# A hybrid GLA and Mamba-2 step: low parts of the weights on VectorE, the decay of the sample states on GpSimd

## The chip, the cores and the metric

The kernel runs on one core of one Trainium2 chip, as one launch. The metric is the device time of an execution in microseconds; for the kernel before it is 1887.03 us, the median of 3 runs (1886.17 to 1887.46).

## The reference

Two layers of a decoder work on 288 tokens at once: a prompt of 256 tokens, and 8 sample sequences of 4 tokens that bring their states with them. Everything is float32. In each layer:

```
x = x + 1/2 * SwiGLU_1(RMSNorm(x))
u = RMSNorm(x);  q,k,v,g,a_lr,z,xbc,dt,gate_a,gate_b = split(u @ w_in)
GLA:  S = decay * S + k_out^T v ;  o = causal(q_in k_in^T) v + q_in S       (4 heads)
SSD:  xs,B,C = silu(causal_conv(xbc)) ; h = decay * h + dS ;                (32 heads, 4 groups)
      y = (C B^T * decays) x dt + C h + d_skip * xs ; y = RMSNorm(y * silu(z))
m = sigmoid(gate_a) * (o_gla @ w_proj_gla) + sigmoid(gate_b) * (y @ w_proj_ssm);  x = x + m @ w_out
x = x + 1/2 * SwiGLU_2(RMSNorm(x))
```

The outputs are the tokens after a last RMSNorm and the new states. The state of a sample in SSD, `state_ssm`, is 64 x 128 for each of 32 heads and 8 sequences; its new value is the old one times exp(sum of dt * A over the 4 tokens), a number per head and sequence, plus a product of the new inputs with B.

## The kernel before

**Weights.** Activations are feature-major: 8 blocks of 128 features by 288 tokens. Every weight comes in pieces of up to 8 blocks of 128 x 128 (`weights`, L169): one DMA on SP's queue into `wr` (four buffers), then `split` (L157) forms a high part `wh` by a copy on ScalarE that rounds to float32r (L160) and a low part `wl` = `wr` - `wh`, a subtraction of 128 x 1024 numbers (three buffers each). The subtraction is done by VectorE (L166) or by GpSimd (L164). Which of the two is decided as the program is written out: `pool_turn` grows by `pool_share` with each piece, and when it reaches 1, one piece goes to GpSimd. `pool_share` is 1.0 in the setup (two pieces), 0.0 in the FFNs and in the projections at the end of the mixer, `SHARE_GLA` = 0.45 in the GLA stage and `SHARE_SSD` = 0.48 in the SSD stage. `mm3` (L176) multiplies a piece: for each block the products of the high part with the high and the low part of the input (L179, L180), and after all of these the low part with the high input (L182).

**Stages of a layer.** FFN, mixer, FFN. The mixer is a generator for the GLA scan and then one for the SSD scan; at each `yield` one step of a list of independent projections (`fillers`, L498: z, g, gate_a with the GLA projection, gate_b) is written between, so that TensorE has products while the chains of the scan run. The engines each run their instructions in order; a scheduler lays the order out when the program is built, so that instructions of different stages mix on an engine.

**The SSD scan** goes over 16 head pairs j (two heads each, 128 rows). The stages that matter here:

- `stage_load(j)` brings the old states of the pair, three pairs ahead: two tiles `st` of 128 x 4 x 128, for even and odd sequences.
- `stage_h` transposes these tiles on TensorE (L144), for C.h.
- `stage_x(j)` projects and convolves the input: copies into `cbuf` (L856 ScalarE, L857 and L858 VectorE), the taps on `cacc` (L861 ScalarE, three times L863 VectorE), tanh and product (L865, L867, L871); GpSimd keeps the last rows (L882, L884).
- `stage_m(j)` makes the inputs token-major, forms the decay-weighted scores `m` (L1015 to L1019 ScalarE, L1029 VectorE), `xg` (L1023 VectorE), `xd` (L1026 GpSimd), and the packed `xpk` (L1031 ScalarE, L1032 VectorE).
- `stage_y(j)` adds the samples' part to `yos` (L1042 VectorE), multiplies outputs and states on TensorE (L1047 to L1054), adds the skip (L1056 VectorE), gates with z on GpSimd (L1062), splits the result (L1064, L1066) and adds its square on GpSimd (L1069). At its end, for both tiles `st`, TensorE forms the new part of the states in a PSUM bank (L1072, from the masked B in `bm`), and VectorE updates the tile in four instructions, one a sequence: old state times its decay `decs` plus the bank (L1076). SP's queue stores it (L1078).
- `stage_group(g)` prepares B and C of four pairs (L928, L931, L936 and others).

The order in which the loop writes them is load(j+3), x(j+2), m(j+1), filler, y(j), filler. The PSUM banks of all these products come from one ring of four (`pst`).

Of the kernel before, what the change touches and what calls it, by code (L numbers as in the profile page):

```python
# [12 lines left out]
ALU = mybir.AluOpType  # L13
# [6 lines left out]
SEQ = 256  # L20
# [21 lines left out]
SHARE_GLA = 0.45  # L42
SHARE_SSD = 0.48
# [3 lines left out]
def _constants():  # L47
    p = np.arange(128)[:, None]
    f = np.arange(128)[None, :]
    ident = (p == f)  # L50
    tri = (f >= p)
    ones = np.ones((128, 128))
    suf = (p > f)
    mid = np.where(f >= 64, (p >= 64) & (p <= f), 0).astype(float) - np.where(f < 64, (p > f) & (p <= 63), 0)
    mid = np.concatenate([mid, (p <= 63), np.ones((128, 1))], 1) / 16.0
    r = p % 32
    c32 = np.arange(32)[None, :]
    ms = np.concatenate([(r // 4 == c32 // 4) & (c32 >= r), r // 4 == np.arange(8)[None, :]], 1) / 16.0
    # packed sample rows: token n in row 32 * (n // 8) + 8 * c + n % 8, for c = 0 .. 3
    tok = lambda a: 8 * (a // 32) + a % 8  # L60
    rep = lambda a: a % 32 // 8
    n, c = tok(p), rep(p)
    seq8 = (n // 4 == np.arange(8)[None, :])
    bt = (c == 0) & (n // 4 == c32 // 4) & (c32 >= n)
    btc = (c < 2) & (n // 4 == c32 // 4) & (c32 >= n)
    sel = (c == 2) & (n == c32)
    bt4 = (c == 0) & (n // 4 == tok(f) // 4) & (n <= tok(f))
    bsuf4 = (c == 0) & (n // 4 == tok(f) // 4) & (n > tok(f))
    pk = np.concatenate([c == 0, c == 1, -1.0 * (c >= 2), -1.0 * (c % 2 == 1), -1.0 * (p % 32 == 1)], 1)
    pair = (p // 2 == np.arange(16)[None, :])  # L70
    par = (p % 2 == f // 64)
    parc = (p % 2 == rep(f))
    parts = dict(ident=ident, pair=pair, tri=tri, ones=ones, seq8=seq8, btc=btc, sel=sel, pk=pk,
                 par=par, parc=parc, suf=suf, mid=mid, ms=ms, bt=bt, bt4=bt4, bsuf4=bsuf4)
    off, cols = {}, 0
    for k, v in parts.items():
        off[k] = (cols, v.shape[1])
        cols += v.shape[1]
    arr = np.concatenate([np.asarray(v, np.float32) for v in parts.values()], 1)
    return np.ascontiguousarray(arr), off  # L80
# [3 lines left out]
NKEEP = COFF["par"][0]          # the columns kept all along; the rest is for GLA and dt  # L84
# [10 lines left out]
def tile_hybrid_step(  # L95
# [21 lines left out]
    def psf():  # L117
        """any of the seven banks of products"""
        turn[0] = (turn[0] + 1) % 7
        return psg() if turn[0] % 2 else ps.tile([128, 512], F32, name="psg", tag="t", bufs=4)[:, 0:NT]  # L120
# [12 lines left out]
    def cz_put(eng, dst, src):  # L133
        """columns of the samples' tokens to the blocks of their sequences; last axes of dst: 264, of src: 32"""
        eng.tensor_copy(out=dst[:, 0:264].rearrange("p (h x) -> p h x", x=132)[:, :, 0:128].rearrange(
            "p h (r c) -> p h r c", c=32)[:, :, :, 16:20], in_=src.rearrange("p (r h t) -> p h r t", h=2, t=4))

    def pack(eng, out, src):
        """[., 32] tokens to the packed order, four times over"""
        eng.tensor_copy(out=out.rearrange("p (r c i) -> p r c i", r=4, c=4),  # L140
                        in_=bcast(src.rearrange("p (r i) -> p r i", i=8), 2, 4))
# [27 lines left out]
    def weights(src):  # L169
        """[n * 128, m <= 128] of DRAM -> the two parts, [128, n, m]"""  # L170
        n, c = src.shape[0] // 128, src.shape[1]
        raw = wpool.tile([128, n, c], F32, name="wr", tag="wr", bufs=4)
        nc.sync.dma_start(out=raw, in_=src.rearrange("(k p) c -> p k c", p=128))
        return split(raw, [128, n, c])
# [9 lines left out]
    def blocks(srcs, x, nblk, first=None, psum=psg, after=1):  # L184
        """per 128-column block: (block, psum of every source); first() follows that many products"""
        for b in range(nblk):
            out = []
            for src in srcs:
                h, lo = early.pop(0) if early else weights(src[:, b * 128:(b + 1) * 128])
                p = psum()  # L190
                mm3(p, h, lo, x[0], x[1], True, True)
                after -= 1
                if first and after == 0:
                    first()
                out.append(p)
            yield b, out

# [10 lines left out]
    def params(l, n1):  # L208
# [18 lines left out]
        # halved: conv_w, conv_b, gla_norm, ssm_norm  # L227
# [11 lines left out]
    class Norm:  # L239
        """RMSNorm of x for the coming phase, fed block by block: x * w split in two; 1 / rms is applied later"""  # L240
# [90 lines left out]
    def mixer(l, P, norm, nxt):  # L331
        W = w_in[l]
        with tc.tile_pool(name="mx", bufs=1) as mx:
# [9 lines left out]
            # the normalised input, split  # L343
# [23 lines left out]
            # conv rows: the samples' 24, the prompt's 3; of each 24 channel blocks  # L367
# [14 lines left out]
            def dt_chain():  # L382
                # dt = softplus(dt_raw + bias), dtA = -dt * exp(a_log); rows are heads
# [20 lines left out]
                # token-major dt, dtA: [tok, (dt|dtA), tile, head]  # L404
# [10 lines left out]
                # cumulative sums within 128-token tiles, suffix sums  # L415
# [9 lines left out]
                # decays to the end: [first tile, second tile, samples]  # L425
# [4 lines left out]
                # head-major cumulative sums, to DRAM for broadcasting  # L430
# [7 lines left out]
                # decay of a sample sequence, on (head, p) partitions  # L438
# [7 lines left out]
                # decays between a sample's tokens, packed rows: of even heads, of odd heads, ones  # L446
# [25 lines left out]
            def fill_g():  # L472
                # output gate of GLA (0.5 folded into gn)
# [38 lines left out]
            pool_share[0] = SHARE_GLA  # L512
            run(gla(l, P, W, norm, X, renorm, dtc, dalt, o8))
            ysq = nacc()
            pool_share[0] = SHARE_SSD
            def proj(yh, conv_store):
                for _ in F:
                    pass
                pool_share[0] = 0.0
# [28 lines left out]
    def gated(wg, X, wp, phs, pls, done):  # L548
        """per output block: done(block, tanh of half the gate, psum of the projection)"""
# [14 lines left out]
    def gla(l, P, W, norm, X, renorm, dtc, dalt, o8):  # L564
        with tc.tile_pool(name="gla", bufs=1) as gp:
# [4 lines left out]
            # both operands of the low-rank product in parts: rows of (x_h, w_l), (x_h, w_h), (x_l, w_h)  # L570
# [8 lines left out]
            # dt and the low-rank decay input  # L579
# [12 lines left out]
            # log_a * 16, token-major  # L592
# [55 lines left out]
            # decays  # L648
# [40 lines left out]
            # sample  # L689
# [19 lines left out]
            # the samples' scores, and the sum of the rows of q.S  # L709
# [4 lines left out]
            # k_out, packed  # L714
# [13 lines left out]
            # prompt states  # L728
# [19 lines left out]
            # outputs, prompt  # L748
# [10 lines left out]
            # sample: outputs and states, two heads at a time  # L759
# [14 lines left out]
            def reads(i):  # L774
                """q.S of four sequences, on a quarter of the columns each"""
# [51 lines left out]
            # per-head RMS: 32 rows of sums per head, broadcast again after 1 / sqrt  # L827
# [19 lines left out]
    def ssd(l, P, W, X, yf, dtt, ac, dec3, eAs, decs, mse, acd, ysq, scf, cbufs, yr, yblk, proj):  # L847
# [3 lines left out]
        with tc.tile_pool(name="ssd", bufs=1) as sp_:  # L851
            def conv(pg, cb, tag, bufs):
                """conv + silu of channel block cb -> compact [128, NT] tile (times 1, weights were halved)"""
# [21 lines left out]
            def bass_sample(a):  # L875
                # the last sequence's group has 4 of 7 columns only
                v = a[:, SEQ + 3 - 3:NCV]          # 56 columns: 3 before, then 8 x (4 + 3)
                return v.rearrange("p (s t) -> p s t", t=7)[:, :, 3:7]

            def conv_last(cb, buf):  # L880
                """last three rows of every sequence, in the old state's place"""
# [12 lines left out]
            R = {}                      # what the stages hand on  # L894
# [3 lines left out]
            def stage_bc(g):  # L898
                """B and C of a group: projection and convolution"""
# [8 lines left out]
            def stage_pack(g):  # L908
                Bf, Cf = R.pop(("bc", g))
                # C of the samples, sequence by sequence  # L910
# [6 lines left out]
            def stage_group(g):  # L917
                """B token-major, C.B, the samples' packed operands"""
# [10 lines left out]
                # C.B  # L929
# [8 lines left out]
                # the samples' score matrices of 4 head pairs, and the sum of the rows of C.h  # L938
# [17 lines left out]
            def stage_load(j):  # L956
                """states of a head pair: even sequences, odd sequences"""
# [4 lines left out]
            def stage_h(hg, i):  # L962
                """C.h of the samples' states"""
# [11 lines left out]
            def stage_h2(hg, i):  # L975
                """C.h, four sequences at a time on a quarter of the columns each"""
# [15 lines left out]
            def stage_x(j):  # L992
                """projection and convolution of a head pair"""
# [9 lines left out]
            def stage_m(j):  # L1003
                """token-major inputs and the decay-weighted scores"""
# [30 lines left out]
            def stage_y(j):  # L1035
                """outputs and new states of a head pair"""
# [3 lines left out]
                y = pst()  # L1040
                for hh in range(2):
# [28 lines left out]
                for hf in range(2):  # L1070
# [3 lines left out]
                    for r in range(4):  # L1074
                        n = 8 * j + 2 * r + hf
                        V.scalar_tensor_tensor(out=sts[hf][:, r], in0=sts[hf][:, r], scalar=decs[:, n:n + 1],  # L1076
                                               in1=p[:, r * 128:r * 128 + 128], op0=ALU.mult, op1=ALU.add)
# [180 lines left out]
```

## Time and profile before

| what | value |
|---|---|
| time, median of 3 runs | 1887.03 us |
| span of the profiled execution | 1883.5 us |
| TensorE busy | 1828.2 us (97%) |
| VectorE busy | 1306.7 us (69%) |
| ScalarE busy | 1032.3 us (55%) |
| GpSimd busy | 347.8 us (18%) |
| DMA | 325.42 MB, mean 173 GB/s |

The profile is of one execution; its page gives the span, from the first to the last instruction, and no other time of that execution. The difference between the span and the median of the timed runs, 3.5 us, lies around the instructions. TensorE's busy time is modelled at the ends of its matmuls, so its gaps say more than its share. GpSimd's work lies in the scan stages (about 222 to 662 us and 1150 to 1590 us) but for the setup.

### The profile page before, as it was taken

How to read it: one execution, taken by the hardware profiler on the slowest of the kernel's cores; microseconds unless marked ns; L12 is line 12 of the kernel's file. 1: busy time of each engine (PE TensorE's matmuls, PEld its weight loads, DVE VectorE, ACT ScalarE, POOL GpSimd, SP SyncE). 2: the span in 40 equal slices, each digit the busy share in tenths (PEclk: the TensorE clock that was granted, in tenths of full speed). 3: DMA queues.
4: the chain of work that ended last, by engine and by line, in shares of the span. 5: the costliest groups of instructions: out<-in, count | busy, mean ns of one | idle time of the engine just before them, and what ended most of it. 6: DMA issues, size and time to landing. Idle time of an engine off the chain costs nothing.

```text
span 1883.5 us, 34917 instructions
## 1 busy us (share of the span) xinstructions
PE 1828.2 (97%) x13712; PEld 1757.0 (93%) x13712; DVE 1306.7 (69%) x2311; ACT 1032.3 (55%) x1818; POOL 347.8 (18%) x324
## 2 busy tenths in 40 slices
PE   8999999998999999999999999999999999999998
PEld 8999998898888899999999999998889898999997
DVE  6555587689888867555565556777988888665554
ACT  6444466565666646444454446565666665454443
POOL 1000032245455300000000001213444452000000
PEclk9999999998999999999999999999989999999999
DMA  7555554866676665555555555569567685555553
GB/s 212 166 164 158 158 154 137 251 184 180 182 202 187 170 179 174 164 169 163 169 167 161 164 164 148 141 193 254 145 168 201 182 220 165 171 159 167 166 157 95
DMA packets 613112, 325.42 MB, mean 173 GB/s; under 512 B 17090, under 2 KB 607986, under 8 KB 612948
## 3 DMA queue, kind: packets, MB, share of 16 engines
q1 hardware_dynamic: 612900, 323.07, 60.1%
q8 instruction: 107, 1.75, 0.4%
q14 instruction: 57, 0.47, 0.1%
q10 hardware_dynamic: 48, 0.13, 0.0%
HBM read 292.93 MB, written 30.22 MB: 172 GB/s over the span
## 4 chain that ended last, share of the span: by engine, by line
PE 49%; DVE 7%; ACT 3%; issue 1%; DMA 1%; POOL 0%; SPq 0%; DVEq 0%; ACTq 0%; POOLq 0%
PE psg L179 15%; PE psg L180 15%; PE psg L182 15%; DVE cacc L863 2%; DVE wl L166 1%; PE pst L144 1%; ACT wh L160 1%; DVE yos L1042 1%; ACT cacc L861 0%; DVE cbuf L858 0%; DMA acb<-acd 0%; DVE st L1076 0%; DVE o L478 0%; PE pst L792 0%; DVE m L1029 0%
## 5 line engine op out<-in xcount | busy, mean ns | idle before, releaser
L160 ACT ACTIVATE wh<-wr 128x1024 fp32r<-128x1024 f32 (+1 forms) x498 | 517.3, 1040 | 449.9 <-PE psg L180 365.6
L179 PE MATMUL psg<-xh,wh 128*128 128x288 f32 x2704 | 748.9, 303 | 9.3 <-DVE cbuf L857 2.7
L180 PE MATMUL psg<-xl,wh 128*128 128x288 f32 x2704 | 742.4, 300 | 0.1
L166 DVE TENSOR_TENSOR wl<-wr,wh 128x1024 fp32r<-128x1024 f32 (+1 forms) x413 | 502.1, 1216 | 126.5 <-ACT wh L160 126.0
L179 PEld LDWEIGHTS psg<-xh,wh 128*128 128x128 f32 x2704 | 514.2, 191 | 16.7 <-issue 6.8
L180 PEld LDWEIGHTS psg<-xl,wh 128*128 128x128 f32 x2704 | 514.9, 191 | 4.4 <-issue 1.9
L182 PE MATMUL psg<-xh,wl 128*128 128x288 f32 x2704 | 415.6, 296 | 0.0
L164 POOL TENSOR_TENSOR wl<-wr,wh 128x1024 fp32r<-128x1024 f32 x85 | 208.3, 2452 | 962.1 <-ACT wh L160 482.1
L182 PEld LDWEIGHTS psg<-xh,wl 128*128 128x128 f32 x2704 | 379.1, 189 | 0.2
L179 PE MATMUL psg<-hh,wh 128*128 128x288 f32 x704 | 189.8, 296 | 0.0
L180 PE MATMUL psg<-hl,wh 128*128 128x288 f32 x704 | 189.5, 295 | 0.0
L306 DVE TENSOR_TENSOR t<-t,psg 128x288 f32<-128x288 f32 x88 | 40.0, 454 | 135.1 <-ACT wh L160 122.9
L180 PEld LDWEIGHTS psg<-hl,wh 128*128 128x128 f32 x704 | 132.6, 188 | 0.0
L179 PEld LDWEIGHTS psg<-hh,wh 128*128 128x128 f32 x704 | 132.2, 188 | 0.1
L863 DVE SCALAR_TENSOR_TENSOR cacc<-cbuf,cw,cacc 128x312 f32<-128x312 f32 x144 | 112.6, 782 | 12.1 <-ACT cacc L861 10.5
L182 PE MATMUL psg<-hh,wl 128*128 128x288 f32 x704 | 109.2, 295 | 0.0
L303 DVE TENSOR_TENSOR t<-psg,rr 128x288 f32<-128x288 f32 x88 | 40.2, 457 | 90.5 <-PE psg L182 90.5
L182 PEld LDWEIGHTS psg<-hh,wl 128*128 128x128 f32 x704 | 99.0, 188 | 0.0
L1076 DVE SCALAR_TENSOR_TENSOR st<-st,decs,pst 128x128 f32<-128x128 f32 x256 | 72.3, 340 | 0.0
L179 PE MATMUL psg<-yh,wh 128*128 128x288 f32 x256 | 69.9, 299 | 0.2
L179 PE MATMUL psg<-oh,wh 128*128 128x288 f32 x256 | 69.7, 299 | 0.0
L180 PE MATMUL psg<-ob,wh 128*128 128x288 f32 x256 | 68.8, 295 | 0.0
(311 smaller groups left out, 2318.2 us busy)
## 6 DMA issues: line engine op xcount, KB each, us to landing
wr<-in_w_ffn_gu_dram SPq DMA_DIRECT2D x176, 512.0 KB
wr<-in_w_in_dram SPq DMA_DIRECT2D x160, 512.0 KB
wr<-in_w_ffn_down_dram SPq DMA_DIRECT2D x64, 448.0 KB
wr<-in_w_ffn_down_dram SPq DMA_DIRECT2D x32, 512.0 KB
st<-in_state_ssm_dram SPq DMA_DIRECT2D x64, 256.0 KB
out_dram<-st SPq DMA_DIRECT2D x64, 256.0 KB
wr<-in_w_proj_ssm_dram SPq DMA_DIRECT2D x32, 512.0 KB
gst<-in_state_gla_dram SPq DMA_DIRECT2D x32, 256.0 KB
```

The lines of the kernel that those rows point to most:

```text
L144: T.transpose(out, in_, ident[0:k, 0:k])
L160: A.activation(out=h, in_=raw, func=AF.Copy)
L164: G.tensor_tensor(out=lo, in0=raw, in1=h, op=ALU.subtract)
L166: V.tensor_tensor(out=lo, in0=raw, in1=h, op=ALU.subtract)
L179: T.matmul(out, lhsT=h[:, k], rhs=xh[k], start=start and k == 0, stop=False)
L180: T.matmul(out, lhsT=h[:, k], rhs=xl[k], start=False, stop=False)
L182: T.matmul(out, lhsT=lo[:, k], rhs=xh[k], start=False, stop=stop and k == n - 1)
L303: V.tensor_tensor(out=t, in0=pg, in1=r, op=ALU.mult)
L306: V.tensor_tensor(out=h, in0=t, in1=pu, op=ALU.mult)
L863: V.scalar_tensor_tensor(out=acc, in0=buf[:, i:i + NCV], scalar=w[i], in1=acc, op0=ALU.mult, op1=ALU.add)
L1042: V.scalar_tensor_tensor(out=yos[:, 2 * (j % 2) + hh], in0=xg[:, 2, 64 * hh:64 * hh + 64], scalar=C["pk"][:, hh:hh + 1], in1=yos[:, 2 * (j ...
L1076: V.scalar_tensor_tensor(out=sts[hf][:, r], in0=sts[hf][:, r], scalar=decs[:, n:n + 1], in1=p[:, r * 128:r * 128 + 128], op0=ALU.mult, op1 ...
```

## The change

Two things. First, the shares are gone: `pool_share` stays 0.0 after the setup, so every low part of the scan stages is formed on VectorE (L166). Second, the update of the sample states is cut in two: at the head of `stage_y` GpSimd multiplies each of the two tiles `st`, 128 x 4 x 128, by the four decays, broadcast along the 128 columns, and after TensorE's product VectorE adds the whole PSUM bank of 512 columns in one instruction instead of four. Comments are also taken out, which has no effect. The core of the diff:

```diff
-SHARE_GLA = 0.45
-SHARE_SSD = 0.48
...
-            pool_share[0] = SHARE_GLA
             run(gla(l, P, W, norm, X, renorm, dtc, dalt, o8))
             ysq = nacc()
-            pool_share[0] = SHARE_SSD
             def proj(yh, conv_store):
                 for _ in F:
                     pass
-                pool_share[0] = 0.0
                 ry = []
...
                 y = pst()
+                for hf in range(2):
+                    G.tensor_tensor(out=sts[hf], in0=sts[hf], in1=bcast(decs[:, 8 * j + hf:8 * j + 8:2], 2, 128), op=ALU.mult)
                 for hh in range(2):
...
                     T.matmul(p, lhsT=xpk, rhs=bm[:, 4 * hf:4 * hf + 4].rearrange("p s d -> p (s d)"),
                              start=True, stop=True)
-                    for r in range(4):
-                        n = 8 * j + 2 * r + hf
-                        V.scalar_tensor_tensor(out=sts[hf][:, r], in0=sts[hf][:, r], scalar=decs[:, n:n + 1],
-                                               in1=p[:, r * 128:r * 128 + 128], op0=ALU.mult, op1=ALU.add)
+                    V.tensor_tensor(out=sts[hf].rearrange("p s d -> p (s d)"), in0=sts[hf].rearrange("p s d -> p (s d)"),
+                                    in1=p, op=ALU.add)
                     nc.sync.dma_start(out=state_view(ssm_s, j, hf), in_=sts[hf])
```

## Rows read from the trace of the kernel before

**Rows 1.** The page's head.

```profile
span 1883.5 us, 34917 instructions
```

**Rows 2.** Windows: stretch, length, busy PE, PEld, DVE, ACT, POOL (instructions), PEclk, DMA.

```profile
222.00:375.00 153.00, 149.69 (x1133) 138.14 (x1132) 110.70 (x211) 93.56 (x167) 38.16 (x22) 0.99 0.61 176
375.00:662.00 287.00, 269.73 (x2029) 248.34 (x2028) 249.63 (x524) 185.31 (x410) 132.42 (x133) 0.97 0.66 185
...
1301.00:1590.00 289.00, 271.73 (x2051) 250.85 (x2051) 253.19 (x527) 185.29 (x410) 132.51 (x135) 0.98 0.68 185
```

**Rows 3.** Groups by line and form; L164 once per SSD stage. Busy, mean | idle before.

```profile
L166 DVE TENSOR_TENSOR wl<-wr,wh 128x1024 fp32r<-128x1024 f32 x348 | 432.0, 1242 | 90.2 <-ACT wh L160 89.7 <-DMA t<-in_ssm_norm_dram 0.5
...
L182 PE MATMUL psg<-xh,wl 128*128 128x288 f32 x2688 | 413.2, 296 | 0.0
...
L863 DVE SCALAR_TENSOR_TENSOR cacc<-cbuf,cw,cacc 128x312 f32<-128x312 f32 x144 | 112.6, 782 | 12.1 <-ACT cacc L861 10.5
...
L1076 DVE SCALAR_TENSOR_TENSOR st<-st,decs,pst 128x128 f32<-128x128 f32 x256 | 72.3, 340 | 0.0
...
L1042 DVE SCALAR_TENSOR_TENSOR yos<-xg,call,yos 128x64 f32<-128x64 f32 x64 | 33.5, 555 | 0.0
...
L858 DVE COPY cbuf<-scf 128x24 f32<-128x24 f32 x48 | 26.8, 561 | 0.9 <-ACT scf L380 0.2
...
L164 POOL TENSOR_TENSOR wl<-wr,wh 128x1024 fp32r<-128x1024 f32 x26 | 64.7, 2489 | 45.8 <-ACT wh L160 38.4 <-ACT cbuf L856 5.9 <-DMA wr<-in_w_proj_gla_dram 1.5
...
L164 POOL TENSOR_TENSOR wl<-wr,wh 128x1024 fp32r<-128x1024 f32 x27 | 67.1, 2484 | 54.6 <-ACT wh L160 54.6
```

**Rows 4.** Single lines: duration ns min/median/max, first and last start.

```profile
L863 DVE SCALAR_TENSOR_TENSOR cacc<-cbuf,cw,cacc x144: 527/543/2673, 377.1 to 1568.4; 128x312 f32<-128x312 f32 x144
...
L1042 DVE SCALAR_TENSOR_TENSOR yos<-xg,call,yos x64: 269/274/2416, 410.3 to 1582.4; 128x64 f32<-128x64 f32 x64
...
L858 DVE COPY cbuf<-scf x48: 171/185/2354, 286.4 to 1536.9; 128x24 f32<-128x24 f32 x48
...
L166 DVE TENSOR_TENSOR wl<-wr,wh x413: 559/1218/3270, 16.3 to 1864.2; 128x1024 fp32r<-128x1024 f32 x113, 128x896 fp32r<-128x896 f32 x24, 128x384 fp32r<-128x384 f32 x1
...
L1076 DVE SCALAR_TENSOR_TENSOR st<-st,decs,pst x256: 328/341/352, 423.3 to 1586.6; 128x128 f32<-128x128 f32 x128
...
L802 DVE TENSOR_TENSOR vs<-vs,gyo x4: 673/679/687, 339.8 to 1281.0; 128x512 f32<-128x512 f32 x4
...
L1026 POOL TENSOR_TENSOR xd<-xg,dec x32: 827/954/1811, 401.8 to 1577.2; 128x384 f32<-128x384 f32 x32
```

**Rows 5.** Timeline at 434 us: start, length, engine, line [idle before].

```profile
434.35 2.59 POOL L164 TENSOR_TENSOR wl<-wr,wh 128x1024 fp32r<-128x1024 f32 x1
...
434.76 2.32 DVE L1032 SCALAR_TENSOR_TENSOR xpk<-xpk,call,xd 128x128 fp32r<-128x128 f32 x1
...
439.10 0.80 PE L1072 MATMUL pst<-bm,xpk 128*128 128x512 f32 x1 [2.74 <-DVE bpk L928]
```

**Rows 6.** Timeline of PE: first and last gap behind a hold.

```profile
229.98 0.46 PE L179 MATMUL psg<-xh,wh 128*48 128x288 f32 x2 [1.05 <-ACT xh L254]
...
1555.41 0.41 PE L1050 MATMUL pst<-msm,yos 128*128 128x32 f32 x2 [1.35 <-DVE yos L1042]
```

**Rows 7.** Windows: four stretches at the lower clock, the first and their sum.

```profile
433.06:443.30 10.24, 7.31 (x31) 5.99 (x27) 9.68 (x22) 6.84 (x20) 5.59 (x6) 0.50 0.55 152
...
sum 27.30, PE 21.95 PEld 20.08 DVE 25.47 ACT 20.69 POOL 11.91; mean PE 5.49 PEld 5.02 DVE 6.37 ACT 5.17 POOL 2.98
```

**Rows 8.** Timeline at 494 us: a product of GpSimd and VectorE beside it.

```profile
493.71 1.06 POOL L1026 TENSOR_TENSOR xd<-xg,dec 128x384 f32<-128x384 f32 x1 [0.32 <-DVE xg L1023]
...
494.01 0.85 DVE L1042 SCALAR_TENSOR_TENSOR yos<-xg,call,yos 128x64 f32<-128x64 f32 x1
```

**Rows 9.** Timeline of the head pair updated at 513 us.

```profile
507.42 0.83 POOL L1026 TENSOR_TENSOR xd<-xg,dec 128x384 f32<-128x384 f32 x1 [0.24 <-DVE xg L1023]
...
513.20 1.12 DVE L1076 SCALAR_TENSOR_TENSOR st<-st,decs,pst 128x128 f32<-128x128 f32 x4
```

## The prediction

> **What bounds the kernel now.** I read the page's busy table first, then the scan stages one by one, then the groups by line, and last the timeline around TensorE's gaps. The execution's span is 1883.5 us [rows 1], 3.5 us under the median of the runs, 1887.03; that lies around the span, and I add it at the end. A change of under 0.2% (3.8 us) cannot be told from none here.
>
> The FFNs don't change, so only four stretches matter: the GLA stages (222 to 375 and 1150 to 1301 us) and the SSD stages (375 to 662 and 1301 to 1590 us) [rows 2]. TensorE sets the time in them, but not alone: it is busy 269.7 of 287 us in the first SSD stage and 271.7 of 289 in the second, and some 3 us of the GLA stage are gaps too (the second GLA stage looks like the first). VectorE is busy 250 of 287 and 253 of 289. A queue that full turns a delay of two microseconds into a gap on TensorE.
>
> Where the delays come from is plain in the groups by line. L1042 handles 64 columns, has a median of 274 ns, and a mean of 555; L858 copies 24 columns, median 185, mean 561; L863 543 against 782; L166 1218 against 1242 [rows 3, 4]. All of them read SBUF twice or copy from SBUF to SBUF. Excess is count times (mean less median): L863 144 x 0.239 = 34.4, L1042 64 x 0.281 = 18.0, L858 48 x 0.376 = 18.0, L166 348 x 0.024 = 8.4, together 78.8 us, nearly all in the SSD stages. L1076, whose second operand is PSUM, never exceeds 352 ns [rows 4]. The timeline shows the holder: GpSimd forms a low part (L164) from 434.35 for 2.59 us, VectorE's L1032 begins at 434.76 and ends with it, 2.32 us later, and TensorE's L1072 then stands idle for 2.74 us [rows 5]. I count fifteen TensorE gaps over 0.6 us that come just behind such a hold by L164, the first at 229 us and the last at 1554 [rows 6]; they sum to 24.1 us, 4.6 of it in the GLA stages. Behind four of the SSD ones the granted clock is 0.50, the 1.2 GHz level, for 27.3 us in which TensorE was busy 21.95 [rows 7]; at 2.4 GHz that work would take half, so 11.0 us are lost. So the SSD stages lose 19.5 + 11.0 = 30.5 us this way, the GLA stages some 5.
>
> **Part 1: the low parts go to VectorE.** In the SSD stages 26 + 27 = 53 leave GpSimd, 131.8 us of it [rows 3]; the others leave in the GLA stages. Each costs VectorE 1.22 us [rows 4], in SSD 64.7 us in all. Their holds go. Of the 78.8 us of excess, part is by other GpSimd work: L1026 holds L1042 to 0.85 us instead of 0.27 [rows 4, 8], 0.58 a time; with 32 of them that is 18.6. Left for L164: 60.2 us, 1.14 each. So the move is nearly even in VectorE's sum. What differs is shape: a hold of up to 2.5 us falls on whatever stands next in the queue, a low part on VectorE is a planned 1.22 us.
>
> What waits behind the moved instruction? VectorE runs in order, and the L166 group already stood idle 89.7 us for ScalarE's high part [rows 3]; conv and score work behind it waits too. But that wait is VectorE standing ahead of TensorE's release of the weights, and TensorE never waited for a low part: L182 shows 0.0 idle [rows 3]. The low part is needed only after sixteen products with the high one. Hence I charge this work less than a hold.
>
> **Part 2: the decay goes to GpSimd.** Removed: 256 of L1076, 72.3 us busy, 1.13 a tile of four [rows 3]. Added on VectorE: 64 additions of 512 columns, one operand in PSUM; L802 is this shape, 0.68 us [rows 4], so 43.5 us, and 28.8 are saved. Added on GpSimd: 64 products of 128x512 with a broadcast factor. That shape is not in the trace; from below L1026's shortest, 0.827 for 384 columns, scaled to 512: 1.10; from above half of L164's 2.49: 1.24. I take 1.15, nearer to L1026, which has a broadcast factor too: 73.6 us in all. Against the 131.8 removed GpSimd still ends with less to do, so its own time is hidden. What isn't hidden is holding VectorE. Bounds: nothing, if they only meet PSUM operands, to 1.15 each, 74 us; the nearest row is L1026's half of its length [rows 8], so 0.58 each, 37 us.
>
> The addition now waits for GpSimd. At 507.42 to 508.25 L1026 of the next head pair runs; two products behind it would end at 510.6, and the first L1076 starts at 513.20 [rows 9]: 2.6 us to spare. Queued behind a late one would be VectorE's next work, a PSUM buffer that TensorE needs, and on SP's queue the store of the state with the next loads behind it. L1062, whose result ScalarE and then VectorE need, now stands behind the two products, but its operand comes at the end of L1056, shortly before 513.20, so I cost that at nothing; if that cover is gone it is in the fourth rival.
>
> Here the Trainium skill speaks against the change. GPSIMD Engine Reference, section Engine selection, says to put elementwise products on VectorE, GpSimd being about twice as slow with two inputs; Perfetto Trace Analysis, section Optimizing Scalar/DVE Operations, adds that the two share a port and moving work between them may not help. The rows agree so far: by them a tile saves 0.45 us of VectorE and is held 0.58. By the rule part 2 is a small loss of 64 x 0.13 = 8 us of VectorE, and part 1 alone would be better than both; this is an estimate.
>
> **The sum.** The SSD stages pay 30.5 us for 78.8 us of hold, 0.39 per us. Holds: -60.2 + 37 = -23.2, times 0.39: -9.0. Work on VectorE: 64.7 - 28.8 = +35.9; charged from nothing (slack) to 0.39 (like a hold, +14.0); I take a quarter, +3.5, since TensorE never waited for a low part but the queue is near full. GLA: VectorE is busy 111 of 153 us there [rows 2], no products are added, and of the 4.6 us of gaps and the slow clock behind one I take 5. Together -9.0 + 3.5 - 5 = -10.5: span 1873.0, time 1876.5; I forecast 1876. What is late next: VectorE itself, in the groups of L863 and L166.
>
> **The rivals.**
> *Work counts like a hold.* The queue is a queue: 1.22 us delay those behind as a hold does. For it: VectorE at 87% of the SSD stages; against it: the zero before L182. Price: -9.0 + 14.0 - 5 = 0: 1887. Chance 0.20.
> *VectorE becomes the bound (slower).* Place: the conv and score chain (L863, L1042, L1032) of each head pair, where the products run back to back behind L1026. They hold in full, 74 us: holds -60.2 + 74 = +13.8, +5.4; work in full +14.0; GLA -5: +14.4, so 1901. For it: L863 and L1042 run in just that stretch; against it: one hold is at most 1.15 instead of 2.5, and L1076 is shorter. It decides from the point at which work counts in full and a product holds more than 0.58. Chance 0.20.
> *All of it comes through.* No new holds and free work: -60.2 x 0.39 - 6 = -30: 1857. It is the forecast's lower end, not a case of its own.
> *The addition is late.* If the 2.6 us are eaten and VectorE waits 1 us in each of 32 head pairs, 32 x 0.39 = +12.5: 1889. Against it: the slack. Chance 0.05.
> That the change would not do what it says I leave out: the share stays 0.0 after the setup (L1163) and no line raises it.
>
> **Chances.** Forecast 0.55, work like a hold 0.20, VectorE bound 0.20, late addition 0.05. The second case spreads by 0.01 to either side, so faster by over 0.2% has 0.56, within 0.2% 0.18 + 0.05 = 0.23, slower 0.21. Alone the forecast spans 1857 (above) to 1883. Eight in ten: 1857 to 1899, which takes in all of the second and fourth cases and part of the third.
>
> **What would show it.** Right: L1042 and L858 fall to means near 0.3 to 0.45 us, longest about 1.4; the gaps before L1072 of 2.5 us and more go, and with them most of the 0.50 stretches; the new product shows 1.1 to 1.25 us; VectorE's busy sum in the SSD stages stays within 20 us of 503. Wrong: gaps of the same sum, now behind L166 or L863; additions waiting for GpSimd; the product far over 1.24 us; or TensorE idle before L182.

## The result, and the profile after

The changed kernel takes 1856.32 us, the median of four runs (1853.35 to 1859.22), against 1886.6 for the kernel before beside it: a ratio of 0.984 (95% interval 0.983 to 0.986), 30.3 us less. That is faster, as forecast, but with three times the gain of the forecast (1876), and 0.7 us outside the range, whose low end was 1857; that is less than the runs differ among themselves.

The page's head and busy line of the changed kernel (for the span, [rows 1]):

```profile
span 1853.4 us, 34776 instructions
...
PE 1816.3 (98%) x13712; PEld 1750.2 (94%) x13712; DVE 1292.0 (70%) x2202; ACT 1035.5 (56%) x1818; POOL 237.1 (13%) x305
```

The span fell by 30.1 us: TensorE's busy time by 11.9 (from 1828.2), its idle time by 18.2 (span less busy, from 55.3 to 37.1). The windows of the first GLA stage and of the two SSD stages, columns as in [rows 2]; the SSD stages now last 273 and 272 us instead of 287 and 289:

```profile
222.00:377.00 155.00, 153.53 (x1163) 141.91 (x1162) 111.55 (x227) 95.09 (x169) 1.94 (x8) 0.99 0.62 179
377.00:650.00 273.00, 262.42 (x2016) 244.02 (x2015) 243.40 (x453) 185.89 (x409) 112.15 (x138) 0.98 0.72 195
1290.00:1562.00 272.00, 262.81 (x2022) 244.19 (x2021) 242.42 (x453) 185.13 (x409) 113.73 (x138) 0.99 0.72 196
```

VectorE's sum in the two SSD stages is 485.8 us; it was 502.8 [rows 2]. In the shorter stretches that is 89% (before: 87%), so the queue is no less full.

The groups by line and form that answer to [rows 3] (L164, L180, L858, L1039, L853 are L166, L182, L863, L1042, L858 of before), with the new product L1037 and the new addition L1071:

```profile
L164 DVE TENSOR_TENSOR wl<-wr,wh 128x1024 fp32r<-128x1024 f32 x430 | 532.1, 1237 | 111.8 <-ACT wh L158 111.1 <-issue 0.2
...
L180 PE MATMUL psg<-xh,wl 128*128 128x288 f32 x2688 | 413.7, 296 | 0.0
...
L858 DVE SCALAR_TENSOR_TENSOR cacc<-cbuf,cw,cacc 128x312 f32<-128x312 f32 x144 | 86.6, 601 | 9.5 <-ACT cacc L856 8.9
...
L1037 POOL TENSOR_TENSOR st<-st,decs 128x512 f32<-128x512 f32 x64 | 83.5, 1323 | 25.5 <-PE pst L142 24.2 <-DMA out_dram<-st 1.3
...
L1071 DVE TENSOR_TENSOR st<-st,pst 128x512 f32<-128x512 f32 x64 | 41.8, 678 | 0.0
...
L1039 DVE SCALAR_TENSOR_TENSOR yos<-xg,call,yos 128x64 f32<-128x64 f32 x64 | 27.8, 460 | 0.0
...
L853 DVE COPY cbuf<-scf 128x24 f32<-128x24 f32 x48 | 17.4, 365 | 0.6 <-ACT scf L378 0.3
```

The means of L858, L1039 and L853 fell by 0.18, 0.10 and 0.20 us. Single lines of the same kernel, as in [rows 4], show what is left of the holds: the longest durations are now 0.88 to 1.34 us instead of 2.35 to 2.67, and what runs beside the longest holds is no longer a low part on GpSimd but a product. Over all of VectorE's lines, no instruction lasts more than 0.89 us over the median of its line.

```profile
L858 DVE SCALAR_TENSOR_TENSOR cacc<-cbuf,cw,cacc x144: 526/539/1336, 377.8 to 1537.6; 128x312 f32<-128x312 f32 x144
...
L1039 DVE SCALAR_TENSOR_TENSOR yos<-xg,call,yos x64: 268/275/876, 413.4 to 1550.2; 128x64 f32<-128x64 f32 x64
...
L853 DVE COPY cbuf<-scf x48: 169/182/1025, 287.2 to 1512.0; 128x24 f32<-128x24 f32 x48
...
L1037 POOL TENSOR_TENSOR st<-st,decs x64: 1037/1249/2138, 396.4 to 1542.0; 128x512 f32<-128x512 f32 x64
```

One such product, in the changed kernel's timeline (columns as in [rows 5]); L476 has a median of 0.51 us, and takes 1.29 here, ending 0.31 us behind the product beside it:

```profile
423.00 1.28 POOL L1037 TENSOR_TENSOR st<-st,decs 128x512 f32<-128x512 f32 x1
423.30 1.29 DVE L476 SCALAR_TENSOR_TENSOR o<-o,prm,ob 128x288 f32<-128x288 f32 x1
```

The 2.74 us gap in front of the state product [rows 5] is gone. TensorE's waits after, largest first (what it waited for, us in total, times, longest), have no entry over 2 us a time but the load at the start. Stretches at granted clock 0.50, the 1.2 GHz level, still occur: four of them, 20.4 us in length, where the kernel before had seven, 37.5 us (a last one, at the end of either program, left out). Their sum after:

```profile
PE psg L142 <- DMA xi<-in_x_prompt_dram: 4.7, 1, 4.7
PE pst L1044 <- DVE xg L1018: 3.7, 4, 1.8
PE pst L926 <- DVE bcf L862: 3.1, 2, 1.9
PE pst L1069 <- ACT sh L967: 2.8, 2, 1.4
```

```profile
sum 20.40, PE 16.74 PEld 15.21 DVE 15.22 ACT 14.24 POOL 5.39; mean PE 4.19 PEld 3.80 DVE 3.81 ACT 3.56 POOL 1.35
```

### The profile page after: what moved, and what is told of

It reads as the page before. It is cut to its first block, busy times and chain, and to the rows that moved or that the text cites. A ratio compares the mean times of both kernels' runs of the same rounds, so it can differ in the third digit from the quotient of the medians.

```text
span 1853.4 us, 34776 instructions
## 1 busy us (share of the span) xinstructions
PE 1816.3 (98%) x13712; PEld 1750.2 (94%) x13712; DVE 1292.0 (70%) x2202; ACT 1035.5 (56%) x1818; POOL 237.1 (13%) x305
## 5 line engine op out<-in xcount | busy, mean ns | idle before, releaser
L164 DVE TENSOR_TENSOR wl<-wr,wh 128x1024 fp32r<-128x1024 f32 (+1 forms) x496 | 602.8, 1215 | 147.9 <-ACT wh L158 147.1
L180 PE MATMUL psg<-xh,wl 128*128 128x288 f32 x2704 | 416.2, 296 | 0.0
L180 PEld LDWEIGHTS psg<-xh,wl 128*128 128x128 f32 x2704 | 378.6, 189 | 1.1 <-issue 0.9
L180 PE MATMUL psg<-hh,wl 128*128 128x288 f32 x704 | 109.2, 296 | 0.0
L180 PEld LDWEIGHTS psg<-hh,wl 128*128 128x128 f32 x704 | 98.9, 188 | 0.0
L858 DVE SCALAR_TENSOR_TENSOR cacc<-cbuf,cw,cacc 128x312 f32<-128x312 f32 x144 | 86.6, 601 | 9.5 <-ACT cacc L856 8.9
L1037 POOL TENSOR_TENSOR st<-st,decs 128x512 f32<-128x512 f32 x64 | 83.5, 1323 | 25.5 <-PE pst L142 24.2
L178 PE MATMUL psg<-yb,wh 128*128 128x288 f32 x256 | 69.2, 297 | 0.8 <-DVE yb L1063 0.8
```

The costliest lines, as they stand in the source:

```text
L164: V.tensor_tensor(out=lo, in0=raw, in1=h, op=ALU.subtract)
L178: T.matmul(out, lhsT=h[:, k], rhs=xl[k], start=False, stop=False)
L180: T.matmul(out, lhsT=lo[:, k], rhs=xh[k], start=False, stop=stop and k == n - 1)
L858: V.scalar_tensor_tensor(out=acc, in0=buf[:, i:i + NCV], scalar=w[i], in1=acc, op0=ALU.mult, op1=ALU.add)
L1037: G.tensor_tensor(out=sts[hf], in0=sts[hf], in1=bcast(decs[:, 8 * j + hf:8 * j + 8:2], 2, 128), op=ALU.mult)
```

## The experiments

The theory: the low parts moved off GpSimd (part 1) gave back more than I had counted, and the decays moved onto GpSimd (part 2) cost something. The first rival: part 2 brings the gain. Times are medians (four runs each, ten for e10), ratios are to the kernel before, whose median lay between 1886.1 and 1886.7.

**e1, part 1 alone** (the kernel before with the shares at nothing).

```diff
-SHARE_GLA = 0.45
-SHARE_SSD = 0.48
+SHARE_GLA = 0.0
+SHARE_SSD = 0.0
```

> The first half alone: both shares 0.0, the state update stays four instructions on VectorE. Theory A (what cost the time are GpSimd's long holds; work planned on VectorE is nearly free there): 60 us of hold go in the SSD stages, at 0.39 us each, so -20 to -24 us: 1863 to 1867 us. Rival B (VectorE's sum counts, hold and work alike): 60 to 75 us of hold go and 65 us of work come, so -4 to +2: 1883 to 1889. Rival C (the gain of the whole change sits in the shorter state update, which frees its PSUM bank sooner): at most -8: 1879 or more.

Measured: 1849.6 us, 0.980 (0.979 to 0.982): 37.0 us less than before, 6.7 less than with both parts. Part 1 is the whole gain and more. Its span and busy line, and its groups as in [rows 3]; under them two groups that I had left out of the count:

```profile
span 1849.2 us, 34842 instructions
...
PE 1819.7 (98%) x13712; PEld 1749.6 (95%) x13712; DVE 1281.6 (69%) x2394; ACT 1035.1 (56%) x1818; POOL 149.4 (8%) x241
```

```profile
L166 DVE TENSOR_TENSOR wl<-wr,wh 128x1024 fp32r<-128x1024 f32 x430 | 526.6, 1226 | 112.0 <-ACT wh L160 111.7
...
L863 DVE SCALAR_TENSOR_TENSOR cacc<-cbuf,cw,cacc 128x312 f32<-128x312 f32 x144 | 83.5, 580 | 9.7 <-ACT cacc L861 9.2
...
L1042 DVE SCALAR_TENSOR_TENSOR yos<-xg,call,yos 128x64 f32<-128x64 f32 x64 | 23.5, 389 | 0.0
...
L858 DVE COPY cbuf<-scf 128x24 f32<-128x24 f32 x48 | 8.6, 183 | 0.5 <-ACT scf L380 0.3
...
L398 DVE SCALAR_TENSOR_TENSOR yb<-yb 32x288 f32<-32x288 f32 x14 | 6.1, 436 | 0.0
...
L140 DVE COPY t<-t 128x128 f32<-128x128 f32 x16 | 3.5, 218 | 0.0
```

The same two groups in the kernel before:

```profile
L140 DVE COPY t<-t 128x128 f32<-128x128 f32 x16 | 14.7, 917 | 0.2
...
L398 DVE SCALAR_TENSOR_TENSOR yb<-yb 32x288 f32<-32x288 f32 x14 | 12.0, 859 | 0.2
```

L863, L1042 and L858 fell by 29.1, 10.0 and 18.2 us, L166 by 348 x 0.016 = 5.6: together 62.9, where I had put 60.2. But the groups that I had left out fell by 47.4 more, a small amount each, L140 (11.2) and L398 (5.9) the largest. So part 1 took some 110 us of holds away, and put 82 x 1.226 = 100.5 us of low parts there (and one small piece of 0.6). The busy line fell by more than the difference, 25.1 us: the records of neighbouring instructions overlap, so sums over groups are good to some 15 us only. The prediction's own measure, mean less median, but over all lines, says the same of the holds: 128.5 us in the kernel before, 21.6 in e1, 57.0 in the changed kernel.

**e2, part 2 alone** (the kernel before, with product and addition as in the change and the shares kept).

```diff
...
+                for hf in range(2):
+                    G.tensor_tensor(out=sts[hf], in0=sts[hf], in1=bcast(decs[:, 8 * j + hf:8 * j + 8:2], 2, 128), op=ALU.mult)
...
-                    for r in range(4):
...
+                    V.tensor_tensor(out=sts[hf].rearrange("p s d -> p (s d)"), in0=sts[hf].rearrange("p s d -> p (s d)"),
+                                    in1=p, op=ALU.add)
```

> The second half alone: the decay on GpSimd and one addition on VectorE, the shares stay 0.45 and 0.48. Theory A: the holds of 64 products (28 to 37 us) come on top of those of the low parts, and the 29 us of work saved are nearly free, so +3 to +12: 1890 to 1899 us. Rival B: 29 us saved against 28 to 37 of hold, so 0 to +3: 1886 to 1890. Rival C: most of the whole change's -30: 1857 to 1868.

Measured: 1909.78 us, 1.013 (1.011 to 1.015), 23.2 us slower: part 2 loses, more so beside the low parts on GpSimd. The page's busy line and TensorE's first wait, in e2; the same wait was 4.6 us in the kernel before:

```profile
PE 1828.1 (96%) x13712; PEld 1755.1 (92%) x13712; DVE 1304.1 (68%) x2119; ACT 1031.7 (54%) x1818; POOL 425.5 (22%) x388
```

```profile
PE pst L144 <- ACT sh L972: 20.5, 13, 3.3
```

VectorE's busy time hardly moved (1306.7 before), so its busy sum doesn't explain the 23 us. The trace shows what stands ahead of the late ScalarE: before 11 of the 13 waits it had itself just been idle, 0.7 to 2.8 us for GpSimd's `xd` (L1026) and 0.6 to 3.2 for VectorE's copy into `cbuf` (L857). Over the whole run these two waits are 57.3 and 56.1 us; they were 49.7 and 41.5. GpSimd's queue, which now holds products and low parts, and the held VectorE both have a share, and no run separates them.

**e3, long holds put back** (the changed kernel, in which GpSimd forms the difference `wr` - `wh` once more behind 48% of the SSD pieces, into a scratch tile that nothing reads; VectorE's own work is unchanged).

```diff
...
+        dturn[0] += dum[0]
+        if dturn[0] >= 1.0:
+            dturn[0] -= 1.0
+            scr = wpool.tile([128, 8, 128], mybir.dt.bfloat16, name="scr", tag="scr", bufs=1)
+            G.tensor_tensor(out=scr[:, 0:shape[1], 0:shape[2]], in0=raw, in1=h, op=ALU.subtract)
         return h, lo
...
```

> The changed kernel, and for 48 of 100 pieces of the SSD stages GpSimd forms the low part a second time into a scratch tile in bfloat16 that nothing reads; VectorE forms the real ones. This brings the holds back (about 53 of 2.4 us) and adds no work to VectorE. Theories A and B alike: 60 to 75 us of hold at 0.39, so +20 to +29 over the changed kernel: 1876 to 1886 us. If holds cost little (rival C): within 8 us of 1856.

Measured: 1960.46 us, 1.039 (1.038 to 1.041), 104 us over the changed kernel. The busy line and the extra group in e3: VectorE, with the same instructions, is busy 100.7 us longer for 167.1 us of GpSimd.

```profile
PE 1848.6 (94%) x13712; PEld 1774.0 (91%) x13712; DVE 1392.7 (71%) x2202; ACT 1034.5 (53%) x1818; POOL 400.3 (20%) x361
```

```profile
L173 POOL TENSOR_TENSOR scr<-wr,wh 128x1024 bf16<-128x1024 f32 x56 | 167.1, 2983 | 160.2 <-ACT wh L162 103.3 <-issue 52.3 <-DMA out_dram<-st 1.2
```

So a microsecond of hold cost 104 / 100.7 = 1.03 us of time, not 0.39. Some 71 us of it are idle time of TensorE and 32 its busy time (1816.3 to 1848.6): 18 stretches, 89 us, have the granted clock 0.50, where the changed kernel has the four of 20.4 us. A rival is that GpSimd frees the weight buffers late. TensorE waited for a weight in these three places only (0.6 us in the changed kernel), so that is a small part at most:

```profile
PE psg L189 <- DVE wl L168: 3.4, 3, 2.3
```

**e4, the work put in twice** (the changed kernel; VectorE forms 56 of the SSD low parts a second time: in e3's diff the last added line becomes the following, and there is no scratch tile).

```diff
+            V.tensor_tensor(out=lo, in0=raw, in1=h, op=ALU.subtract)
```

> The changed kernel, and for 48 of 100 pieces of the SSD stages VectorE forms the same low part twice over: about 53 more instructions of 1.2 us, 64 us of work on VectorE, and no hold. Theory A: nearly free, +0 to +7 over the changed kernel: 1856 to 1863 us. Rival B: 64 x 0.39 = +25: 1881 us. A result between 1866 and 1876 would say that work counts at a part of the price of a hold, as the forecast's quarter did.

Measured: 1906.03 us, 1.010 (1.008 to 1.011), 50 us over the changed kernel. The extra group took 72.6 us; under it, TensorE's waits for a low part, of which the changed kernel has none:

```profile
L172 DVE TENSOR_TENSOR wl<-wr,wh 128x1024 fp32r<-128x1024 f32 x56 | 72.6, 1297 | 0.1
...
PE psg L188 <- DVE wl L172: 12.7, 13, 1.8
...
PE psg L188 <- DVE wl L168: 5.7, 7, 1.0
```

That is 0.69 us of time per us of work: neither nothing nor as much as a hold. It is not the price of a fuller queue alone, though: the second subtraction (L172) writes `wl` once more, and the products wait 12.7 us for it. Without these it is 0.51.

**e5, holds without the tie to the weights** (as e3, but GpSimd subtracts two parts of a tile of the input, `xt`, so that no weight buffer waits for it).

```diff
...
-            G.tensor_tensor(out=scr[:, 0:shape[1], 0:shape[2]], in0=raw, in1=h, op=ALU.subtract)
+            G.tensor_tensor(out=scr.rearrange("p a b -> p (a b)"), in0=xt.rearrange("p a b -> p (a b)")[:, 0:1024],
+                            in1=xt.rearrange("p a b -> p (a b)")[:, 1024:2048], op=ALU.subtract)
```

> As the extra hold, but GpSimd's extra subtraction reads 2 x 1024 columns of the residual stream, which nothing writes in this stage, so it delays the release of no weight buffer. Theory A (what costs is VectorE held off SBUF, about 1 us of time per us of hold): again far over the changed kernel, +70 to +110: 1926 to 1966 us. Rival D (in the run before the cost was the late release of the weights' buffers to the DMA and to ScalarE): within 25 us of 1856.

Measured: 1933.02 us, 1.026 (1.024 to 1.027), 77 us over the changed kernel, with VectorE busy 97.9 us longer: 0.78 per us. But with no weight to wait for, these instructions ran early, back to back, from 228 to 311 and from 1178 to 1261 us, all of them in the GLA stages. So the run has no say on the buffers in e3's SSD stages (the first of these, from its first tap on `cacc` to its last skip addition, takes 262.0 us here and 263.6 in the changed kernel). It says something else: holds packed into a GLA stage cost almost as much, although VectorE is busy only 111 of 155 us there in the changed kernel. The window of the first GLA stage in e5, and the groups that were hit, steps of one chain on 32 rows (437 and 298 ns in the changed kernel):

```profile
222.00:375.00 153.00, 125.79 (x861) 116.01 (x861) 133.11 (x179) 73.79 (x134) 81.83 (x34) 0.87 0.43 121
```

```profile
L405 DVE SCALAR_TENSOR_TENSOR yb<-yb 32x288 f32<-32x288 f32 x14 | 32.1, 2292 | 0.0
...
L399 DVE TENSOR_SCALAR yb<-yb 32x288 f32<-32x288 f32 x2 | 5.0, 2500 | 0.0
```

**e6, GpSimd work that reads no SBUF** (as e3, with two fills of the scratch tile in place of the subtraction).

```diff
...
+            for _ in range(2):
+                G.memset(scr, 0.0)
...
```

> As the extra hold, but instead of the subtraction GpSimd fills the scratch tile with zeros twice: it is busy and reads nothing. Theory A with holds by whatever GpSimd does: in proportion to the fills' length, +30 or more for 1 us each. Theory A with holds by reads only: VectorE's instructions with two SBUF operands keep their medians beside a fill, only copies from SBUF to SBUF can be held, so 0 to +12: 1856 to 1868 us. Rival D: 0.

Measured: 1855.31 us, 0.984 (0.983 to 0.985): nothing against the changed kernel, for 106.6 us of GpSimd. Tied to nothing, though, all the fills ran between 2 and 119 us, in the first FFN, so this says little of the SSD stages. e12 mends that.

**e7, part 1 in the SSD stages alone** (the kernel before with `SHARE_SSD = 0.0`, `SHARE_GLA` kept).

> The kernel before with the share of the SSD stages at 0.0 and that of the GLA stages left at 0.45. The forecast gave the GLA stages 5 of the gain: then 1854 to 1856 us against 1849.6 with both at 0.0. Rival E (VectorE is busy 111 of 153 us in the GLA stages, so TensorE catches up by itself and a hold there costs nothing): 1847 to 1852.

Measured: 1857.36 us, 0.985 (0.983 to 0.986): 28.8 us less than before. That is what the share of the SSD stages is worth; e1 gains 7.8 us more, the worth of the GLA stages' share. 56 pieces of 128x1024 moved here (404 on VectorE, 348 before), and mean less median over all lines fell from 128.5 to 53.0 us, so 75.5 us of holds went, and another 31.4 with the GLA stages' share in e1:

```profile
L166 DVE TENSOR_TENSOR wl<-wr,wh 128x1024 fp32r<-128x1024 f32 x404 | 493.9, 1224 | 101.1 <-ACT wh L160 98.6 <-PE pst L144 2.2
```

**e8, the decay on ScalarE** (e1, with the 256 products as activations with a scale; VectorE adds the whole bank, as in the change).

```diff
...
+                for hf in range(2):
+                    for r in range(4):
+                        n = 8 * j + 2 * r + hf
+                        A.activation(out=sts[hf][:, r], in_=sts[hf][:, r], func=AF.Copy, scale=decs[:, n:n + 1])
...
```

> All low parts on VectorE, and the decay as four ScalarE instructions a tile (256 in all) in place of GpSimd's product; VectorE only adds. Theory A: no hold comes and 29 us of work go, at 0.7 us each, so -15 to -20 from 1849.6: 1830 to 1835 us, if ScalarE's queue (186 of 273 us in an SSD stage, and 38 us more) takes it. Rival F: ScalarE becomes the late engine in the chain cbuf, cacc, tanh: 1850 to 1875.

Measured: 1840.47 us, 0.976 (0.975 to 0.977), the best of all: 46 us under the kernel before, 16 under the changed one. VectorE is busy 21.8 us less than in e1 (1259.8), for 9.1 us of time: 0.42 per us. Whether the price of work falls as the queue empties, or ScalarE's new work takes part of the gain back, no run separates. The decays take 87.6 us of ScalarE (its busy line rises by 64.4, 1035.1 to 1099.5), and next to nothing is held: VectorE's other groups rise by 2.1 us in all against e1. The decays and the additions:

```profile
L1044 ACT ACTIVATE st<-st,decs 128x128 f32<-128x128 f32 x256 | 87.6, 393 | 0.0
...
L1078 DVE TENSOR_TENSOR st<-st,pst 128x512 f32<-128x512 f32 x64 | 41.8, 678 | 0.0
```

**e9 and e10, a third of e4 and of e3** (the same diffs with 18 extra instructions instead of 56).

> The changed kernel, with the doubled VectorE low part for 16 of 100 pieces of the SSD stages instead of 48: about 18 instructions, 22 us of work. If work counts in proportion (50 us of time for 65 us above): +15 to +18: 1871 to 1874 us. If it counts only beyond the point at which VectorE is full (theory A with a threshold): +0 to +7: 1856 to 1863.

> The changed kernel, with GpSimd's extra subtraction for 16 of 100 pieces instead of 48, about 18 of it: if holds count in proportion (104 us for 53 to 56 above): +33 to +37: 1889 to 1893 us. If a hold costs little while VectorE still has room: +0 to +15: 1856 to 1871.

Measured: 1868.4 us, 0.990 (0.988 to 0.991), and 1889.26, 1.001 (1.000 to 1.002): 12 and 33 us over the changed kernel, about a quarter and a third of e4's and e3's. The extra groups of e9 (with TensorE's waits for a low part) and of e10:

```profile
L172 DVE TENSOR_TENSOR wl<-wr,wh 128x1024 fp32r<-128x1024 f32 x18 | 23.9, 1330 | 0.0
...
PE psg L188 <- DVE wl L168: 8.4, 5, 5.2
...
PE psg L188 <- DVE wl L172: 3.2, 2, 2.0
```

```profile
L173 POOL TENSOR_TENSOR scr<-wr,wh 128x1024 bf16<-128x1024 f32 x18 | 56.2, 3121 | 35.5 <-ACT wh L162 32.6 <-issue 2.3 <-POOL cz L136 0.5
```

The price per us of work is 0.5 here, or 0.4 without the wait for L172; VectorE is busy 29.0 us longer in e10 (1321.0), 1.1 per us of hold. At a third of the amount neither is free; less was not tried.

**e11, half of the decay on ScalarE** (e8 for the even sequences' tile, VectorE's four instructions for the other).

> All low parts on VectorE; of each head pair's two state tiles one is decayed on ScalarE and added whole on VectorE, the other stays four instructions on VectorE. If VectorE's work sets the pace and ScalarE has room, half of the 9 us gained with both: 1844 to 1846 us. If ScalarE's 38 us more in each stage cost something back there, this is the better balance: 1834 to 1840.

Measured: 1842.87 us, 0.977 (0.975 to 0.978): 6.7 of e8's 9.1 us come with the first half; the 2 us over one half are within the spread of the runs.

**e12, the fills in place** (e6, and ahead of the two fills ScalarE writes one column of the scratch tile).

```diff
...
+            A.activation(out=scr[:, 0, 0:1], in_=h[:, 0, 0:1], func=AF.Copy)
             for _ in range(2):
                 G.memset(scr, 0.0)
...
```

> The changed kernel, where behind 48% of the pieces of the SSD stages ScalarE writes one column of a scratch tile from the high part, and GpSimd then fills that tile with zeros twice (some 112 fills of 0.95 us, 107 us; the tile is used by nothing). The one column ties the fills to the SSD stages; in the run before without it all of them ran in the first FFN. Theory that only GpSimd instructions which read SBUF hold VectorE: VectorE's busy time stays within 4 us of 1292, and the time within 8 us above 1856 (what the 56 small ScalarE writes may cost), 1856 to 1864. Rival, that any GpSimd instruction holds VectorE: as with the extra subtractions, 0.6 us for each us of GpSimd, VectorE's busy time up by some 60 us and the time 1910 to 1930.

Measured: 1855.3 us, 0.983 (0.982 to 0.985), no change against the changed kernel, with VectorE busy 1290.6. The fills now ran from 369 to 1528 us, inside the SSD stages:

```profile
L175 POOL MEMSET scr<- x112: 945/952/1030, 368.6 to 1527.6; 128x1024 bf16 x112
```

So it is not GpSimd's being busy that holds VectorE, but its reading of SBUF; the readers tried all had two inputs. The Trainium skill has this rule (SBUF — State Buffer, section Who interferes with whom): a VectorE instruction with two SBUF inputs contends with GpSimd instructions that read SBUF, not with those that only write. e3 and e12 agree, with 100.7 us of hold for the reads and none for the writes.

## Why the prediction was right and wrong

**What bounds the kernel: right.** TensorE was held up by VectorE, and VectorE by GpSimd. e1 takes GpSimd's low parts away and TensorE's idle time falls from 55.3 to 29.5 us; e3 puts reads of that kind back and loses 104.

**Where the 20 us lie.** By e7, e1 and the changed kernel, the parts of the sum were forecast and measured as follows:

| part | forecast | measured |
|---|---|---|
| low parts of the SSD stages: -60.2 x 0.39 + a tenth of 64.7 | -17.2 | -28.8 (e7) |
| low parts of the GLA stages | -5 | -7.8 (e1 against e7) |
| the decay: 37 x 0.39 less a tenth of 28.8 | +11.6 | +6.7 (after against e1) |

**The step that failed is the price in the sum:** "The SSD stages pay 30.5 us for 78.8 us of hold, 0.39 per us". The 30.5 us are gaps and slow stretches behind holds by L164 alone; the 78.8 us include the 18.6 of L1026 as well. Over L164's own 60.2 us the price would have been 0.51, and the first term -30.5 instead of -23.5: 7.0 of the 20 us. Another 6.3 are the charge for the work and 4.9 the decay. With all of L164's gaps given back and the work at nothing, the prediction's reading comes to -30.5 - 5 = -35.5, and e1 gained 37.0 (span: 25.8 us less idle on TensorE, 8.5 less busy).

That agreement is luck, since neither the price of 0.51 nor the free work stands the test. Put back one amount at a time, holds cost 0.8 to 1.1 us per us (e3, e5, e10), and work, for which I charged 0.10, measured 0.7 and 0.5 (e4, e9; 0.5 and 0.4 without the waits for the part written twice). And the four lines were too few: they lost 62.9 us for 60.2 forecast (e1), the lines that I had put at nothing another 47.4, most of it in the GLA stages (75.5 us of holds go in e7, 31.4 more in e1). So the gaps just behind a hold showed too little of what holds cost, by about what the work takes back. With 1.03 and 0.69, e7's 75.5 us of holds and 56 x 1.224 = 68.5 us of work come to -30.5; with 0.8 and 0.5 to -26; for -28.8 measured. Mixed pairs give -13 to -43, so this is no proof, and how the difference is shared between price and count stays open. For part 2 the second pair gives +13.7, for +6.7 measured, so its short holds cost less than long ones, or its work more.

"TensorE never waited for a low part" was no reason for a low price, although L182 (L180 after) still shows 0.0 idle. In e4 and e9 the queue is fuller and TensorE does wait for low parts written once (L168: 5.7 and 8.4 us); that in the changed kernel it is the work behind the low part that comes late is argued, not shown.

**The GLA stages:** 5 us forecast, 7.8 measured (e7 against e1). "VectorE is busy 111 of 153 us" seemed slack; e5 shows that holds packed there cost 0.78 per us, and the lines hit most are steps of one chain. The 5 us had no term for the 26 low parts that VectorE gets there, 26 x 1.226 = 32 us; they about equal the 31.4 us of holds that go.

**Part 2: right in sign, too dear by 4.9 us.** Work out and in: 73.6 - 41.8 = 31.8 us saved (28.8 forecast). Holds: VectorE's other groups rose by 37.0 us from e1 to the changed kernel, the 64 x 0.58 forecast, but by luck: the product takes 1.32 us, past the bound of 1.24, and less of it than half is a hold. So by groups VectorE gets 5.2 us more to do (by the busy lines 10.4, 1281.6 to 1292.0), and the time rises by 6.7. By its own prices my sum implied +11.6 (37 x 0.39 for the holds less 28.8 x 0.10 for the work). The rule that I set beside it (the Trainium skill, GPSIMD Engine Reference, Engine selection), with its consequence that part 1 alone beats both, is borne out by e1: 1849.6 against 1856.3.

**The rivals.** Work that counts like a hold: its half that work isn't free is right, its price of 0.39 and so its 1887 are not. VectorE as the bound, 1901: no; the products held as much as the forecast had, half of the rival's 74. The late addition: L1071 shows 0.0 idle ahead of it, so it never waited for GpSimd. "All of it comes through", 1857 (it puts 6 us on the GLA stages where the sum has 5), is nearest in its number, and that is luck too: it has no new holds and free work, and the runs show 37 us of new holds and work that is paid. e1 passed it by 7 us.

**The signs.** L853 (0.365) is within the 0.3 to 0.45 named and L1039 (0.460) just above; their longest are 1.03 and 0.88 us, under the 1.4 named; the gap of 2.7 us is gone, and VectorE's SSD sum is 17 us under 503. The product, 1.32 us, is just over the 1.1 to 1.25 named. Most of the slow stretches were to go: of seven, four are still there.

## What to carry to other kernels

Where one engine's queue is near 90% full, price a change in that engine's time by adding a little and measuring, not by the gaps that can be tied to a cause: here each us of hold cost about 1 us and each us of planned work 0.4 to 0.7. Let the added work write nothing that others wait for, or its price holds that wait too (e4), and check in the trace in which stage it ran (e5, e6). Divide a loss only by the causes that it was counted for. Sum mean less median over all lines, the small ones too: here the lines left out held 47 us, three quarters of what the four largest did. Elementwise work that must leave VectorE goes better to an engine that doesn't hold it: on ScalarE the same decays, 87.6 us of them, gained 9 us where on GpSimd they lost 7.

## What was not expected of the hardware

A VectorE instruction of TENSOR_SCALAR kind, with one input tile, was held about as long as those with two: L399 of e5, 2500 ns instead of 298. Copies from SBUF to SBUF are held as well, not only the small L858 of the prediction (L140: 917 ns before, 218 in e1). Two of the price's details stay open: why part 2 costs 23 us beside the low parts on GpSimd and 7 without them, and why a us of hold costs 0.8 us in e5 and 1.0 to 1.1 in e3 and e10.
